# The last matrix product of a decoder layer: eight block products, or seven with sums of blocks

## The chip, the cores and the metric

One NeuronCore of a Trainium2 chip runs the whole program. TensorE (PE) does the matrix products and has a separate row of the profile for its weight loads (PEld); VectorE (DVE) and ScalarE (ACT) do the elementwise work; GpSimd (POOL) does little here, and SyncE (SP) issues most of the DMA transfers. The metric is the device time of one execution in microseconds (us): the median over the runs.

## The reference

One layer of a decoder with 512 positions and 1024 channels, in fp32. Four mixers give one 512-channel branch each. What follows them matters here:

```python
merged = jnp.sum(jax.nn.sigmoid(mg.reshape(B, S, N_BRANCHES, D)) * proj, axis=2)
return x + merged @ w_out
```

`mg` are gate columns of the input projection, `proj` the four branches after their own projection. `merged` is 512x1024, `w_out` 1024x1024. The products are to have nearly the accuracy of fp32.

## The kernel before

**Three matmuls for one.** Each operand of a matrix product is split into a rounded part `hi` (fp32r) and the rest `lo`; a product is hi\*hi + lo\*hi + hi\*lo, three matmuls. For a block of weights this costs a cast on ACT (`hi_cast`, L159) and a subtraction on DVE (L175, L1254 or L1396).

**The gates as seven products.** For the last three branches, `merge(n, ...)` computes the gate columns with the generator `seven()` (L1257). It cuts both operands into 2x2 blocks and replaces the eight block products by seven, of sums and differences of blocks. The sums of weight blocks are made by DVE in `add` (L1304, target `tsum` or a block that is no longer needed). Six PSUM banks hold what accumulates (`x`, `z`, `y`, two each): `seed` copies bank x to bank y on ACT, `less` (L1296) subtracts y from a kept copy `c` into z on DVE, `after_s3` does so again (L1299). A product is 24 matmuls. With `early` true (branch 2) the product of block 12 with block 21 of the weights comes second, so that it lies between the first product and the first one that needs a sum. Two more matmuls open bank y. Behind each gate comes `project()` (L1022): 2 x 96 matmuls into bank pairs `pj`, after which DVE multiplies by the gate (`th`, L1341) and adds to `acc` (L1342). The order of branches is 2, 1, 3.

**The output projection.** `acc` is turned by 32 transposes on PE (`turn`, L1383) through banks `tr`; ACT writes `mh` (L1386), DVE writes `ml` (L1387). Eight weight half-blocks of 1024 columns (`wo_split`) are split one by one, and `out_step` (L1405 to L1407) issues 192 matmuls of 128x512, first for the left half of the columns, then for the right. The rows of `x` come in eight DMAs of 256 KB on ACT's queue (`residual`, L1411). For every finished bank DVE adds them (L1415), and SP stores the result (L1416).

**What sets the order.** Generators hand out work in small steps (`yield`), `run` and `fill` take steps from them, and a scheduler orders the instructions of each engine. Each engine then works through its own list strictly in order. A raw block of weights has a limited number of slots (four under `raw`, five under `raw2`), so a load starts when an earlier block has been read.

Of the kernel before, what the change touches and what calls it, by code (L numbers as in the profile page):

```python
# [9 lines left out]
F32 = mybir.dt.float32  # L10
F32R = mybir.dt.float32r
# [50 lines left out]
def f32(ap):  # L62
    return ap.bitcast(F32)
# [3 lines left out]
def tile_hybrid_layer(ctx: ExitStack, tc: tile.TileContext, x, xT, units, small, bsp, out):  # L67
# [1067 lines left out]
    def sg_mix(dq):  # L1135
        wsh, wsl, bs, vnh, vnl = sg_setup(dq)
        for p_ in range(4):
            for b2 in range(2):
# [4 lines left out]
                for bb in range(2):  # L1143
# [5 lines left out]
                mx = accp.tile([P, S], F32, tag="tm", bufs=3, name=f"mx{p_}{b2}")[:, 0:256].rearrange("p (b t) -> p b t", b=2)  # L1149
# [9 lines left out]
    tmp_pool[:] = [accp, "tm"]  # L1159
    cnt["act"] = 0  # L1160
    later(*silu("gc", y["c"], (1, 3)), merge_plain(0, y["a"]))
    for i in range(4):
# [41 lines left out]
    def x_ops():  # L1204
# [11 lines left out]
        c = mp.tile([P, 1024], F32, name="xs").rearrange("p (k s) -> p k s", k=4)  # L1216
# [27 lines left out]

    def blocks(n):

        return {c: [half(*at, f"mg{n}{int(c[1]) - 1}.{int(c[0]) - 1}", h) for h in range(2)]
                for c, at in (("11", (wp, "raw", 4)), ("21", (wp, "raw", 4)), ("12", (mq, "raw2", 5)),
                              ("22", (mq, "raw2", 5)))}

    def weights(name, raw):
        w = wpair(name, 0)
# [4 lines left out]
    def seven(raws, ops, kt, emit, nm, early, beside):  # L1257

        nh = kt // 2
        b12, b11, b21, b22 = (raws[c] for c in ("12", "11", "21", "22"))  # L1260
        acc_ = {w: [zbank(f"{nm}{w}{p}") for p in range(2)] for w in "xzy"}
        cb = {}

        def product(w, op, src, first, then, made=None):
            hi_op, lo_op = ops[op]
            for h in range(nh):
                wt = made[h] if made else weights(f"{nm}{w}{op}", src[h])
# [17 lines left out]

        def seed(p, ps):
            if len(opened) < 2:
                opened.append(PE.matmul(acc_["y"][p], lhsT=xh[:, 0, 0:P], rhs=xh[:, 0, :], start=True, stop=True))
            ACT.copy(acc_["y"][p], ps)

        def keep(p, ps):
            cb[p] = accp.tile([P, S], F32, tag="th", bufs=4, name=f"{nm}c{p}")
            ACT.copy(cb[p], ps)

        def less(p, ps):
# [8 lines left out]
                DVE.tensor_tensor(dst[h], a[h], b[h], op=ALU.add)  # L1304

        def c11():
            return product("x", "12", b21, False, lambda p, ps: emit(p, 0, ps))
# [19 lines left out]
    def merge(n, yt, ths, first=False):  # L1327
# [16 lines left out]
        yield from seven(head if first else blocks(n), xo, 4, gate, f"mg{n}", first, y_split())  # L1344
        for c in range(2):
            yield from project(n, c, yh, yl, add)

# [10 lines left out]
    dqs.close()  # L1358
    mq = pool("mq")
    cnt["act"] = 1  # L1360
    head = blocks(2)
    head["w"] = [weights("mg2", raw) for raw in head["11"]]
    run(xg)
    drain()
# [1 line left out]
    psum_close("z")  # L1366
    psum_open("z")
    ps_["nz"] = 8
    ths = [tile8("th0"), ylp.tile([P, 4, S], F32, tag="vd", bufs=1, name="th1")]
# [7 lines left out]
    def turn(tp):  # L1377

        for kk in range(4):
            b = zbank(f"tr{tp}{kk}").rearrange("p (k t) -> p k t", k=2)  # L1380
            for k in range(2):
                for t in range(2):
                    PE.transpose(b[:, k, t * P:(t + 1) * P],  # L1383
                                 acc[:, 2 * tp + t, (2 * kk + k) * P:(2 * kk + k + 1) * P], identf)
            at = (slice(None), slice(2 * kk, 2 * kk + 2), slice(256 * tp, 256 * tp + 256))
            ACT.activation(mh[at], b, AF.Copy, scale=0.25)  # L1386
            DVE.scalar_tensor_tensor(ml[at], b, 0.25, f32(mh[at]), op0=ALU.mult, op1=ALU.subtract)  # L1387

    def wo_split(c, q):
        raw = half(*((wp, "raw", 4) if q % 2 else (mq, "raw2", 5)), f"wo{c}.{q // 2}", q % 2)  # L1390
        if c == 0 and q < 3:
            w = mp.tile([P, 2, 1024], F32R, tag=("s1", "s2", "s4")[q], bufs=1, name=f"wo{q}")
        else:
            w = wpair(f"wo{c}", q)
        hi_cast(w[:, 0, :], raw)
        DVE.tensor_tensor(w[:, 1, :], raw, f32(w[:, 0, :]), op=ALU.subtract)  # L1396
        return w[:, 0, :], w[:, 1, :]

    def out_step(pos, w, q, t):
        hi, lo = w  # L1400
        ts_ = slice(t * P, (t + 1) * P)
        for k2 in range(2):
            k = 2 * q + k2
            ws = slice(k2 * S, (k2 + 1) * S)
            PE.matmul(pos, lhsT=mh[:, k, ts_], rhs=hi[:, ws], start=k == 0, stop=False)  # L1405
            PE.matmul(pos, lhsT=ml[:, k, ts_], rhs=hi[:, ws], start=False, stop=False)  # L1406
            PE.matmul(pos, lhsT=mh[:, k, ts_], rhs=lo[:, ws], start=False, stop=k == KD - 1)  # L1407

    def residual(c, t):
        r = accp.tile([P, S], F32, tag="th", bufs=4, name=f"xr{c}{t}")  # L1410
        nc.scalar.dma_start(r, x[t * P:(t + 1) * P, c * S:(c + 1) * S])  # L1411
        return r

    def store(c, t, pos, r):
        DVE.tensor_tensor(r, pos, r, op=ALU.add)  # L1415
        DMA.dma_start(out[t * P:(t + 1) * P, c * S:(c + 1) * S], r)  # L1416

    turn(0)
    ws_ = {}
    for c in range(2):  # L1420
        pos = [zbank(f"out{c}{t}") for t in range(4)] if c else []
        xr_ = [residual(c, t) for t in range(4)]
        if c == 0:
            for tp in range(2):
                pos += [zbank(f"out0{2 * tp + t}") for t in range(2)]
                for q in range(4):
                    if tp == 0:
                        ws_[q] = wo_split(0, q)
                    for t in (2 * tp, 2 * tp + 1):
                        out_step(pos[t], ws_[q], q, t)  # L1430
                    if tp == 0 and q == 0:
                        turn(1)
                for t in (2 * tp, 2 * tp + 1):
                    store(0, t, pos[t], xr_[t])
        else:
            for q in range(4):
                w = wo_split(1, q)
                for t in range(4):
                    out_step(pos[t], w, q, t)
            for t in range(4):  # L1440
                store(1, t, pos[t], xr_[t])
    psum_close("z")


# [81 lines left out]
```

## Time and profile before

| | |
|---|---|
| time, median of 3 runs | 746.86 us (745.25 to 747.06) |
| the profiled execution | 745.62 us |
| its span, first to last instruction | 743.7 us |
| PE busy | 718.1 us, 97% of the span |
| DVE busy | 547.0 us, 74% |
| ACT busy | 356.6 us, 48% |
| last projection, 670.69 to 692.45 us | PE busy 21.76 of 21.76 us |
| output projection, 692.45 to 740.05 us | PE busy 47.60 of 47.60 us, DVE 15.27, ACT 7.18 |
| from there to the end | 3.65 us |

The profiled execution took 1.92 us beside its span and is 1.24 us under the median. Matmuls overlap: one of 128x512 is shown with about 0.39 us and starts about 0.23 us after the one before, so the distance of the starts tells what it costs.

### The profile page before, as it was taken

Reading aid. Unit: us, or ns where it says so; the run is one execution under the profiler, and the core shown is the slowest. Engines: PE = TensorE matmul, PEld = TensorE weight load, DVE = VectorE, ACT = ScalarE, POOL = GpSimd, SP = SyncE. Lnnn points to the kernel's source line nnn. Section 1 sums busy time; section 2 is a strip of 40 time slices with the busy share of each in tenths; the row PEclk is TensorE's granted clock in tenths of the full one; section 3 lists DMA queues with packets and bytes.
Section 4 is the critical chain, followed back from the end, with each engine's and each line's share of the span. In section 5 each row is a group of like instructions: output and inputs, shape, how many; then the busy total and the mean of one; then the engine's idle time right before and its main releaser. Section 6 shows DMA issues by size and latency. Waiting matters only on the chain.

```text
span 743.7 us, 9597 instructions
## 1 busy us (share of the span) xinstructions
PE 718.1 (97%) x3387; PEld 575.3 (77%) x3387; DVE 547.0 (74%) x1014; ACT 356.6 (48%) x731; POOL 185.5 (25%) x235
## 2 busy tenths in 40 slices
PE   8999999988999999999999999999999999999998
PEld 6878777766777787777777677788788888888886
DVE  5798757877568547978687999899768858965622
ACT  4422655655644136766576592433552551663210
POOL 5253644364444113233325333100000000000000
PEclk9999999999999999999999999999999999999999
DMA  8622311111113431100101133225432243143031
GB/s 312 216 69 101 115 56 58 57 57 58 63 51 105 151 113 57 58 30 29 57 30 32 55 113 100 85 85 198 134 122 85 83 140 111 65 141 112 0 114 56
DMA packets 20496, 68.35 MB, mean 92 GB/s; under 512 B 2400, under 2 KB 2528, under 8 KB 20448
## 3 DMA queue, kind: packets, MB, share of 16 engines
q1 hardware_dynamic: 19008, 65.28, 25.8%
q10 hardware_dynamic: 1440, 2.46, 1.0%
q8 instruction: 26, 0.43, 0.2%
q14 instruction: 22, 0.18, 0.1%
HBM read 65.64 MB, written 2.10 MB: 91 GB/s over the span
## 4 chain that ended last, share of the span: by engine, by line
PE 65%; DVE 17%; issue 7%; ACT 5%; POOL 5%; DMA 1%; SPq 0%; POOLq 0%; ACTq 0%; DVEq 0%
PE tb L573 3%; PE pj L1034 3%; PE pj L1035 3%; PE pj L1036 3%; PE out L1405 2%; PE out L1406 2%; PE out L1407 2%; PE o_s L586 1%; PE o_s L587 1%; PE z_va L212 1%; PE z_va L210 1%; DMA xr<-in_xT_dram 1%; PE z_va L211 1%; PE z_xb L189 1%; PE z_xb L190 1%
## 5 line engine op out<-in xcount | busy, mean ns | idle before, releaser
L1034 PE MATMUL pj<-w_wb,yh 128*128 128x512 f32 x128 | 49.9, 390 | 0.9 <-ACT tm L1006 0.9
L1035 PE MATMUL pj<-w_wb,yl 128*128 128x512 f32 x128 | 49.8, 389 | 0.0
L1036 PE MATMUL pj<-w_wb,yh 128*128 128x512 f32 x128 | 49.8, 389 | 0.0
L578 ACT CAST ph_a<-tb 128x256 fp32r<-128x256 f32 x40 | 14.8, 371 | 32.5 <-PE tb L573 30.1
L579 DVE TENSOR_TENSOR pl_a<-tb,ph_a 128x256 fp32r<-128x256 f32 x40 | 16.9, 421 | 17.1 <-ACT ph_a L578 16.9
L1034 PEld LDWEIGHTS pj<-w_wb,yh 128*128 128x128 f32 x128 | 24.0, 188 | 6.3 <-ACT tm L1006 1.3
L175 DVE TENSOR_TENSOR w_wb<-r_wb,w_wb 128x1024 fp32r<-128x1024 f32 x16 | 19.5, 1221 | 12.4 <-ACT w_wb L159 12.4
L1036 PEld LDWEIGHTS pj<-w_wb,yh 128*128 128x128 f32 x128 | 24.0, 188 | 5.1
L1035 PEld LDWEIGHTS pj<-w_wb,yl 128*128 128x128 f32 x128 | 24.0, 188 | 4.9
L562 POOL TENSOR_SCALAR p_w<-p_w,nm_w 128x128 f32<-128x128 f32 (+3 forms) x32 | 19.0, 612 | 31.8 <-DVE nm_w L559 18.1
L1415 DVE TENSOR_TENSOR xr<-out,xr 128x512 f32<-128x512 f32 x8 | 5.5, 692 | 27.1 <-PE out L1407 27.1
L562 POOL TENSOR_SCALAR p_s<-p_s,nm_s 128x128 f32<-128x128 f32 (+3 forms) x32 | 16.5, 533 | 35.6 <-DVE nm_s L559 21.7
L562 POOL TENSOR_SCALAR p_a<-p_a,nm_a 128x128 f32<-128x128 f32 (+3 forms) x32 | 20.2, 650 | 6.9 <-DVE nm_a L557 4.9
L579 DVE TENSOR_TENSOR pl_s<-tb,ph_s 128x256 fp32r<-128x256 f32 x40 | 16.3, 418 | 6.5 <-ACT ph_s L578 6.4
L578 ACT CAST ph_s<-tb 128x256 fp32r<-128x256 f32 x40 | 14.3, 371 | 13.5 <-PE tb L573 13.4
L554 ACT ACTIVATE p_w<-p_w,nm_w 128x512 f32<-128x512 f32 (+3 forms) x32 | 17.9, 561 | 5.9 <-DVE nm_w L552 5.8
L579 DVE TENSOR_TENSOR pl_w<-tb,ph_w 128x256 fp32r<-128x256 f32 x40 | 16.3, 421 | 5.9 <-ACT ph_w L578 5.5
L573 PE MATMUL tb<-identf,p_a 128*128 128x128 f32 x80 | 16.1, 281 | 3.7 <-DVE pl_a L579 1.6
L554 ACT ACTIVATE p_a<-p_a,nm_a 128x512 f32<-128x512 f32 (+3 forms) x32 | 17.8, 556 | 4.0 <-DVE nm_a L552 3.8
L578 ACT CAST ph_w<-tb 128x256 fp32r<-128x256 f32 x40 | 14.2, 371 | 10.9 <-PE tb L573 10.2
L159 ACT CAST w_wb<-r_wb 128x1024 fp32r<-128x1024 f32 x12 | 12.6, 1048 | 13.4 <-PE pj L1036 10.8
L554 ACT ACTIVATE p_s<-p_s,nm_s 128x512 f32<-128x512 f32 (+3 forms) x32 | 17.8, 559 | 2.1 <-DVE nm_s L552 2.1
(910 smaller groups left out, 2514.8 us busy)
## 6 DMA issues: line engine op xcount, KB each, us to landing
r_wb<-in_units_dram SPq DMA_DIRECT2D x16, 512.0 KB, 3.5
xt<-in_x_dram SPq DMA_DIRECT2D x4, 512.0 KB, 8.0
r_ga<-in_units_dram SPq DMA_DIRECT2D x4, 512.0 KB, 3.5
r_gd<-in_units_dram SPq DMA_DIRECT2D x4, 512.0 KB, 3.6
r_ud<-in_units_dram SPq DMA_DIRECT2D x4, 512.0 KB, 3.6
r_gc<-in_units_dram SPq DMA_DIRECT2D x4, 512.0 KB, 3.5
r_xb<-in_units_dram SPq DMA_DIRECT2D x4, 512.0 KB, 3.5
r_gb<-in_units_dram SPq DMA_DIRECT2D x4, 512.0 KB, 3.7
```

The lines of the kernel that those rows point to most:

```text
L175: DVE.tensor_tensor(w[:, 1, :], raw, f32(w[:, 0, :]), op=ALU.subtract)
L554: ACT.activation(pi, pi, AF.Exp, scale=-1.0, bias=nm[:, i:i + 1], accum_out=nm[:, 4 + i:5 + i])
L562: POOL.tensor_scalar(pi, pi, nm[:, 8 + i:9 + i], 0.0, op0=ALU.mult, op1=ALU.add)
L573: PE.transpose(t_[:, c * P:(c + 1) * P], u.p[:, OFF[i] + j * P:OFF[i] + (j + 1) * P], identf)
L578: ACT.copy(ph[:, c:c + 256], t_)
L579: DVE.tensor_tensor(pl_[:, c:c + 256], t_, f32(ph[:, c:c + 256]), op=ALU.subtract)
L1034: PE.matmul(banks[t], lhsT=yh[:, k, ts_], rhs=hi[:, cs], start=k == 0, stop=False)
L1035: PE.matmul(banks[t], lhsT=yl[:, k, ts_], rhs=hi[:, cs], start=False, stop=False)
L1036: PE.matmul(banks[t], lhsT=yh[:, k, ts_], rhs=lo[:, cs], start=False, stop=k == 3)
L1405: PE.matmul(pos, lhsT=mh[:, k, ts_], rhs=hi[:, ws], start=k == 0, stop=False)
L1406: PE.matmul(pos, lhsT=ml[:, k, ts_], rhs=hi[:, ws], start=False, stop=False)
L1407: PE.matmul(pos, lhsT=mh[:, k, ts_], rhs=lo[:, ws], start=False, stop=k == KD - 1)
```

## The change

The output projection goes through `seven()` with the four 512x512 blocks of `w_out` (`blocks("wo")`) and with the blocks of the merged result. For that:

- Per bank of the transposes the kernel keeps the merged values in fp32 as well (`mt`, `m21`), forms `s1`, `m3`, `s2` and `s4` as sums and differences of blocks, and splits each into an operand pair (`pair`: ACT copy, DVE subtraction).
- The sums of weight blocks are made as for the gates, four pairs of 1024-column additions.
- The blocks 11 and 21 of `w_out` are split during the last `project`; 21 goes to two slots of its own, and `run(last_merge, ...)` sets after which steps.
- The eight tiles of the output are emitted by the products in the order in which they are finished.
- The rows of `x` are fetched by eight DMAs on SP's queue into the slots of the last branch's operand (`res`).
- The pool of `th` and `tm` is closed before the gates, and one for the copies `c` opened in its place.

```diff
     thc.close()
+    keepp = pool("keepp", side="right")
...
-    for n, yt in ((2, y["c"]), (1, y["b"]), (3, ug)):
+    for n, yt in ((2, y["c"]), (1, y["b"])):
         run(merge(n, yt, ths, n == 2))
+    last_merge = merge(3, ug, ths)
+    run(last_merge, 56 + 16 + 9)
+    wraw = blocks("wo")
+    wraw["w"] = [weights("wo11", raw) for raw in wraw["11"]]
+    run(last_merge, 2)
+    wraw["w21"] = [weights("wo21", wraw["21"][0], ylp.tile([P, 2, 1024], F32R, tag="z8", bufs=1, name="w_wo21"))]
+    run(last_merge, 2)
+    wraw["w21"].append(weights("wo21", wraw["21"][1], keepp.tile([P, 2, 1024], F32R, name="w_wo21h1")))
+    run(last_merge)
...
+    for c, t0 in ((0, 0), (1, 2), (1, 0), (0, 2)):
+        for t in (t0, t0 + 1):
+            DMA.dma_start(res[c][:, t, :], x[t * P:(t + 1) * P, c * S:(c + 1) * S])
...
+    def pair(nm, src, w):
+        hi, lo = (w[:, j, :].rearrange("p (k s) -> p k s", k=4) for j in range(2))
+        ACT.copy(hi, src)
+        DVE.tensor_tensor(lo, src, f32(hi), op=ALU.subtract)
+        mo[nm] = (hi, lo)
...
+    lowb = [turn(0, kk, bank) for kk, bank in enumerate(tb + ob["z"])]
+    highb = [turn(1, kk, bank) for kk, bank in enumerate(ob["y"])]
+    for kk in range(4):
+        turn_split(0, kk, lowb[kk])
+    for kk in range(2):
+        ACT.activation(mt[:, at2[kk], :], lowb[kk], AF.Copy, scale=0.25)
+    for kk in range(2):
+        ACT.activation(m21[:, at2[kk], :], highb[kk], AF.Copy, scale=0.25)
+
+    def store(t, c, src):
+        r = res[c][:, t, :]
+        DVE.tensor_tensor(r, src, r, op=ALU.add)
         DMA.dma_start(out[t * P:(t + 1) * P, c * S:(c + 1) * S], r)
...
+    go = seven(wraw, mo, 4, store, "wo", True, iter(()), ob)
+    run(go, 1)
+    highb = [turn(1, 2 + kk, bank) for kk, bank in enumerate(tb)]
+    for kk in range(2):
+        DVE.scalar_tensor_tensor(s1[:, at2[kk], :], highb[kk], -0.25, m21[:, at2[kk], :], op0=ALU.mult, op1=ALU.add)
+    pair("s1", s1, operand("s1"))
+    for kk in range(2):
+        ACT.activation(mt[:, at2[2 + kk], :], lowb[2 + kk], AF.Copy, scale=0.25)
+        turn_split(1, 2 + kk, highb[kk])
+    run(go, 9)
+    DVE.tensor_tensor(m3, m11, m21, op=ALU.subtract)
+    DVE.tensor_tensor(m11, s1, m11, op=ALU.subtract)
+    pair("s2", m11, operand("s2"))
+    run(go, 12)
+    pair("s3", m3, mid("ms3"))
+    run(go, 8)
+    DVE.tensor_tensor(m12, m12, m11, op=ALU.add)
+    pair("s4", m12, operand("s4"))
+    run(go)
```

The functions `wo_split`, `out_step` and `residual`, and the loop that calls them, go. In `seven()` the subtraction `less` is L1299 after the change (L1296 before), the sums are L1307, the splits L1256.

Three places in the order of the instructions. The first is DVE's list during the last `project`, before the change (`w_wb` are the weights that this projection still needs, `wo` those of the output):

```order
L175 TENSOR_TENSOR w_wb_5990<-r_wb_5988,w_wb_5990 128x1024 [waits DMAHW7_49,PE_49,Activation_49]
L1396 TENSOR_TENSOR wo_6141<-r_wo0.01_6139,wo_6141 128x1024 [waits DMAHW6_49,Activation_49]
L175 TENSOR_TENSOR w_wb_6019<-r_wb_6017,w_wb_6019 128x1024 [waits DMAHW0_49,Activation_49]
L1341 SCALAR_TENSOR_TENSOR th_4848<-th_4848,pj_5914 128x512 [waits PE_49]
L1341 SCALAR_TENSOR_TENSOR th_4848<-th_4848,pj_5915 128x512 [waits PE_49]
```

and after it:

```order
L1307 TENSOR_TENSOR tsum<-r_wo0.00_6032,r_wo1.00_6040 128x1024 [waits DMAHW6_49,DMAHW2_49]
L175 TENSOR_TENSOR w_wb_5997<-r_wb_5995,w_wb_5997 128x1024 [waits DMAHW5_49,PE_49,Activation_49]
L1307 TENSOR_TENSOR tsum<-r_wo0.01_6034,r_wo1.01_6042 128x1024 [waits DMAHW7_49,DMAHW3_49]
L1307 TENSOR_TENSOR r_wo1.00_6040<-r_wo1.00_6040,r_wo1.10_6044 128x1024 [waits DMAHW0_49,DVE_49]
L1307 TENSOR_TENSOR r_wo1.01_6042<-r_wo1.01_6042,r_wo1.11_6046 128x1024 [waits DMAHW1_49,DVE_49]
L175 TENSOR_TENSOR w_wb_6026<-r_wb_6024,w_wb_6026 128x1024 [waits DMAHW6_49,Activation_49]
L1344 SCALAR_TENSOR_TENSOR th_4855<-th_4855,pj_5921 128x512 [waits PE_49]
```

Four additions that wait for loads of `w_out` (DMAHW) now stand ahead of the last split that the projection needs and ahead of the first gate multiplication.

The second place is PE's list at the start of the output projection, before:

```order
L1383 MATMUL tr_6077<-identf,acc 128x128 x4
L1405 MATMUL out_6092<-wo_6096,mh 128x512 [waits Activation_49]
L1405 MATMUL out_6093<-wo_6096,mh 128x512
L1383 MATMUL tr_6111<-identf,acc 128x128 [waits DVE_49]
L1383 MATMUL tr_6111<-identf,acc 128x128 x2
L1406 MATMUL out_6092<-wo_6096,ml 128x512 [waits DVE_49]
```

and after (the banks `outz` and `outy` serve as transpose banks first):

```order
L1405 MATMUL outy_6101<-identf,acc 128x128 x4
L1279 MATMUL outx_6096<-w_wo_6048,mh 128x512 [waits DVE_49,Activation_49]
L1281 MATMUL outx_6096<-w_wo_6048,ml 128x512 [waits DVE_49]
L1283 MATMUL outx_6096<-w_wo_6048,mh 128x512
L1279 MATMUL outx_6096<-w_wo_6048,mh 128x512
L1405 MATMUL tr_6094<-identf,acc 128x128 [waits Activation_49]
```

24 instead of 16 transposes stand ahead of the first matmul of the product, and the last eight, which write the first two banks a second time, wait for ACT.

The third place is DVE's list in the output projection, after the change, up to the subtraction `less` (`ms` are the operand pairs, `w_woys` the split sums of weight blocks, `woc` the kept copy):

```order
L1417 TENSOR_TENSOR ms_6256<-m_6093,ms_6256 128x1024
L1438 TENSOR_TENSOR resh<-outx_6097,resh 128x512 [waits DMAHW0_49,PE_49]
L1307 TENSOR_TENSOR tsum<-tsum,r_wo1.10_6044 128x1024 [waits DVE_49]
L1307 TENSOR_TENSOR tsum<-tsum,r_wo1.11_6046 128x1024 [waits DVE_49]
L1458 TENSOR_TENSOR mt<-mt 128x1024
L1256 TENSOR_TENSOR w_woys_6269<-tsum,w_woys_6269 128x1024 [waits Activation_49]
L1256 TENSOR_TENSOR w_woys_6284<-tsum,w_woys_6284 128x1024 [waits Activation_49]
L1417 TENSOR_TENSOR ms_6295<-mt,ms_6295 128x1024 [waits Activation_49]
L1307 TENSOR_TENSOR tsum<-tsum,r_wo0.10_6036 128x1024 [waits DVE_49]
L1307 TENSOR_TENSOR tsum<-tsum,r_wo0.11_6038 128x1024 [waits DVE_49]
L1299 TENSOR_TENSOR outz_6098<-woc_6254,outy_6100 128x512 [waits PE_49]
L1299 TENSOR_TENSOR outz_6099<-woc_6265,outy_6101 128x512 [waits PE_49,Activation_49]
```

Before the change this stretch of DVE's list held eight `ml`, three splits and the additions of the residual rows; now 25 operations stand between the last `acc` addition and `less`, 10 of 512 elements (six `ml`, two into `mu`, two residual additions) and 15 of 1024. SP's list has the eight loads of `x` behind all loads of `w_out` and ahead of the stores.

## Rows read from the trace of the kernel before

**Rows 1.** The page's part 1: busy time, share of span, instructions.

```profile
PE 718.1 (97%) x3387; PEld 575.3 (77%) x3387; DVE 547.0 (74%) x1014; ACT 356.6 (48%) x731; POOL 185.5 (25%) x235
```

**Rows 2.** Busy time by stretch: branch 2's gates, last projection, output projection; columns ahead.

```profile
core 0: us, PE busy (x) PEld busy (x) DVE busy (x) ACT busy (x) POOL busy (x), PEclk, DMA share, GB/s
511.68:550.99 39.31, 38.93 (x171) 31.76 (x170) 29.83 (x30) 21.17 (x26) 0.00 (x0) 1.00 0.35 118
670.69:692.45 21.76, 21.76 (x97) 17.97 (x96) 13.77 (x18) 5.65 (x6) 0.00 (x0) 1.00 0.23 80
692.45:740.05 47.60, 47.60 (x225) 39.31 (x223) 15.27 (x22) 7.18 (x11) 0.00 (x0) 1.00 0.16 55
```

**Rows 3.** Timeline of PE, output stage's start: start, duration, instruction, count.

```profile
692.22 0.39 PE L1036 MATMUL pj<-w_wb,yh 128*128 128x512 f32 x1
692.45 1.91 PE L1383 MATMUL tr<-identf,acc 128*128 128x128 f32 x16
694.25 0.73 PE L1405 MATMUL out<-wo,mh 128*128 128x512 f32 x2
```

**Rows 4.** Timeline of PE and DVE at the end; in brackets, idle time and releaser.

```profile
739.43 0.39 PE L1406 MATMUL out<-w_wo,ml 128*128 128x512 f32 x1
...
739.66 0.39 PE L1407 MATMUL out<-w_wo,mh 128*128 128x512 f32 x1
740.09 0.69 DVE L1415 TENSOR_TENSOR xr<-out,xr 128x512 f32<-128x512 f32 x1 [0.67 <-PE out L1407]
```

**Rows 5.** Timeline of PE: branch 2's gates begin, their projection begins.

```profile
511.68 0.39 PE L1277 MATMUL mg2x<-w_mg,xh 128*128 128x512 f32 x1
...
551.01 0.39 PE L1034 MATMUL pj<-w_wb,yh 128*128 128x512 f32 x1
```

**Rows 6.** Timeline around branch 2's subtraction `less`.

```profile
533.76 1.29 DVE L1296 TENSOR_TENSOR mg2z<-mg2c,mg2y 128x512 f32<-128x512 f32 x2
...
534.57 0.19 PEld L1277 LDWEIGHTS mg2y<-w_mg2ys,xs 128*128 128x128 f32 x1 [0.78 <-issue]
534.60 0.47 PE L1277 MATMUL mg2y<-w_mg2ys,xs 128*128 128x512 f32 x1 [0.38 <-DVE mg2z L1296]
```

**Rows 7.** Timeline of ACT and DVE as the output projection begins.

```profile
693.26 1.29 DVE L1342 TENSOR_TENSOR acc<-acc,th 128x512 f32<-128x512 f32 x2
...
693.61 2.04 ACT L1386 ACTIVATE mh<-tr 128x512 fp32r<-128x512 f32 x4
...
694.46 2.48 DVE L1387 SCALAR_TENSOR_TENSOR ml<-tr,mh 128x512 fp32r<-128x512 f32 x4
```

**Rows 8.** Timeline of DVE in branch 2's gates.

```profile
519.09 0.69 DVE L1333 TENSOR_TENSOR yl<-y_c,yh 128x512 fp32r<-128x512 f32 x1
519.69 1.22 DVE L1254 TENSOR_TENSOR w_mg2zs<-tsum,w_mg2zs 128x1024 fp32r<-128x1024 f32 x1
520.94 1.22 DVE L1304 TENSOR_TENSOR tsum<-tsum,r_mg21.10_4781 128x1024 f32<-128x1024 f32 x1
```

**Rows 9.** Timeline of DVE in branch 1's projection, which began at 610.85.

```profile
612.02 1.22 DVE L1304 TENSOR_TENSOR tsum<-r_mg30.00_5648,r_mg31.00_5656 128x1024 f32<-128x1024 f32 x1 [1.39 <-DMA r_mg30.00_5648<-in_units_dram]
...
614.96 1.23 DVE L1304 TENSOR_TENSOR tsum<-r_mg30.01_5650,r_mg31.01_5658 128x1024 f32<-128x1024 f32 x1 [0.57 <-DMA r_mg30.01_5650<-in_units_dram]
616.10 1.22 DVE L1304 TENSOR_TENSOR r_mg31.00_5656<-r_mg31.00_5656,r_mg31.10_5660 128x1024 f32<-128x1024 f32 x1
617.24 1.22 DVE L1304 TENSOR_TENSOR r_mg31.01_5658<-r_mg31.01_5658,r_mg31.11_5662 128x1024 f32<-128x1024 f32 x1
...
619.51 1.28 DVE L1341 SCALAR_TENSOR_TENSOR th<-th,pj 128x512 f32<-128x512 f32 x2
```

**Rows 10.** Timeline of DVE in the last projection, which began at 670.69.

```profile
678.56 1.28 DVE L1341 SCALAR_TENSOR_TENSOR th<-th,pj 128x512 f32<-128x512 f32 x2
```

**Rows 11.** DMA issues from 560 us on: KB each, median us to landing.

```profile
r_mg30.00_5648<-in_units_dram SPq DMA_DIRECT2D x1, 512.0 KB, 3.5
...
r_wo1.00_6260<-in_units_dram SPq DMA_DIRECT2D x1, 512.0 KB, 6.1
```

More of the change, by code (lines that the diff above doesn't have):

```diff
@@ L996, in tile_hybrid_layer @@
     acc = accp.tile([P, 4, D], F32, name="acc")
+    thc = ExitStack()
+    thp = pool("thp", thc, side="right")
     def merge_plain(n, yt):
@@ L1157, in sg_mix @@
                 yield 0.8
-    tmp_pool[:] = [accp, "tm"]
+    tmp_pool[:] = [thp, "tm"]
     cnt["act"] = 0
@@ L1245, in blocks, with weights @@
     def blocks(n):
-        return {c: [half(*at, f"mg{n}{int(c[1]) - 1}.{int(c[0]) - 1}", h) for h in range(2)]
+        return {c: [half(*at, f"{n}{int(c[1]) - 1}.{int(c[0]) - 1}", h) for h in range(2)]
                 for c, at in (("11", (wp, "raw", 4)), ("21", (wp, "raw", 4)), ("12", (mq, "raw2", 5)),
                               ("22", (mq, "raw2", 5)))}
-    def weights(name, raw):
-        w = wpair(name, 0)
+    def weights(name, raw, w=None):
+        w = wpair(name, 0) if w is None else w
         hi_cast(w[:, 0, :], raw)
@@ L1255, in weights, with seven @@
         return w
-    def seven(raws, ops, kt, emit, nm, early, beside):
+    def seven(raws, ops, kt, emit, nm, early, beside, banks=None):
         nh = kt // 2
         b12, b11, b21, b22 = (raws[c] for c in ("12", "11", "21", "22"))
-        acc_ = {w: [zbank(f"{nm}{w}{p}") for p in range(2)] for w in "xzy"}
+        acc_ = banks or {w: [zbank(f"{nm}{w}{p}") for p in range(2)] for w in "xzy"}
         cb = {}
@@ L1266, in product @@
             for h in range(nh):
-                wt = made[h] if made else weights(f"{nm}{w}{op}", src[h])
+                wt = made[h] if made and h < len(made) else weights(f"{nm}{w}{op}", src[h])
                 hi, lo = wt[:, 0, :], wt[:, 1, :]
@@ L1287, in seed @@
             if len(opened) < 2:
-                opened.append(PE.matmul(acc_["y"][p], lhsT=xh[:, 0, 0:P], rhs=xh[:, 0, :], start=True, stop=True))
+                opened.append(PE.matmul(acc_["y"][p], lhsT=ops["11"][0][:, 0, 0:P], rhs=raws["w"][0][:, 0, 0:S], start=True,
+                                        stop=True))
             ACT.copy(acc_["y"][p], ps)
         def keep(p, ps):
-            cb[p] = accp.tile([P, S], F32, tag="th", bufs=4, name=f"{nm}c{p}")
+            cb[p] = keepp.tile([P, S], F32, tag="kept", bufs=3, name=f"{nm}c{p}")
             ACT.copy(cb[p], ps)
@@ L1306, in c11 @@
         def c11():
-            return product("x", "12", b21, False, lambda p, ps: emit(p, 0, ps))
+            return product("x", "12", b21, False, lambda p, ps: emit(p, 0, ps), raws.get("w21"))
         t_ = [tsum[:, h, :] for h in range(nh)]
@@ L1342, in add @@
             DVE.tensor_tensor(a, a, th, op=ALU.add)
-        yield from seven(head if first else blocks(n), xo, 4, gate, f"mg{n}", first, y_split())
+        yield from seven(head if first else blocks(f"mg{n}"), xo, 4, gate, f"mg{n}", first, y_split())
         for c in range(2):
@@ L1360, in tile_hybrid_layer @@
     cnt["act"] = 1
-    head = blocks(2)
+    head = blocks("mg2")
     head["w"] = [weights("mg2", raw) for raw in head["11"]]
@@ L1374, in tile_hybrid_layer @@
+    run(last_merge, 2)
+    wraw["w21"].append(weights("wo21", wraw["21"][1], keepp.tile([P, 2, 1024], F32R, name="w_wo21h1")))
+    run(last_merge)
     mh = xp.tile([P, KD, S], F32R, tag="xh", bufs=1, name="mh")
     ml = xp.tile([P, KD, S], F32R, tag="xl", bufs=1, name="ml")
[L1377 to L1415, printed above, removed]
-        DMA.dma_start(out[t * P:(t + 1) * P, c * S:(c + 1) * S], r)
[L1418 to L1441, printed above, removed]
@@ new lines, in tile_hybrid_layer @@
+    mt, mu = (tile8(nm)[:].rearrange("p a (b s) -> p (a b) s", b=2) for nm in ("mt", "mu"))
+    m3 = mp.tile([P, 1024], F32, tag="xs", bufs=1, name="m3").rearrange("p (k s) -> p k s", k=4)
+    m11, m12, m21, s1 = mt[:, 0:4, :], mt[:, 4:8, :], mu[:, 0:4, :], mu[:, 4:8, :]
+    tb = [zbank(f"tr{j}") for j in range(2)]
+    ob = {w: [zbank(f"out{w}{p}") for p in range(2)] for w in "xzy"}
+    res = [accp.tile([P, 4, S], F32, tag="y" + w, bufs=1, name=f"res{w}") for w in "hl"]
+    for c, t0 in ((0, 0), (1, 2), (1, 0), (0, 2)):
+        for t in (t0, t0 + 1):
+            DMA.dma_start(res[c][:, t, :], x[t * P:(t + 1) * P, c * S:(c + 1) * S])
@@ new lines, in turn, with turn_split @@
+    def turn(tp, kk, bank):
+        b = bank.rearrange("p (k t) -> p k t", k=2)
+        for k in range(2):
+            for t in range(2):
+                PE.transpose(b[:, k, t * P:(t + 1) * P],
+                             acc[:, 2 * tp + t, (2 * kk + k) * P:(2 * kk + k + 1) * P], identf)
+        return b
+    def turn_split(tp, kk, b):
+        at = (slice(None), slice(2 * kk, 2 * kk + 2), slice(256 * tp, 256 * tp + 256))
+        ACT.activation(mh[at], b, AF.Copy, scale=0.25)
+        DVE.scalar_tensor_tensor(ml[at], b, 0.25, f32(mh[at]), op0=ALU.mult, op1=ALU.subtract)
@@ new lines, in pair, with operand @@
+    def pair(nm, src, w):
[3 more added lines that the diff above has]
+        mo[nm] = (hi, lo)
+    def operand(nm):
+        return mp.tile([P, 2, 1024], F32R, tag=nm, bufs=1, name="m" + nm)
+    k1, k2 = slice(0, 4), slice(4, 8)
+    mo = {"11": (mh[:, k1, LOW], ml[:, k1, LOW]), "12": (mh[:, k2, LOW], ml[:, k2, LOW]),
+          "22": (mh[:, k2, HIGH], ml[:, k2, HIGH])}
@@ new lines, in tile_hybrid_layer @@
+    at2 = [slice(2 * kk, 2 * kk + 2) for kk in range(4)]
+    lowb = [turn(0, kk, bank) for kk, bank in enumerate(tb + ob["z"])]
[9 more added lines that the diff above has]
+        DVE.tensor_tensor(r, src, r, op=ALU.add)
+        DMA.dma_start(out[t * P:(t + 1) * P, c * S:(c + 1) * S], r)
```

10 lines of the change are left out of this document (6 added, 4 removed).

## The prediction

> **What bounds the kernel now.** I read the page's busy shares first. PE is busy for 97% of the span, DVE for 74% [rows 1]; whatever the change does, it must show in PE's list. The shares are an average, so the second view is the busy time by stretch [rows 2]: in the output projection PE works 47.60 of 47.60 us, with DVE at 15.27 and ACT at 7.18; in the projection ahead of it 21.76 of 21.76, with DVE at 13.77. The granted clock is 1.00 in all of them, so a matmul has one price. That price comes from the stretch of the last projection: 96 matmuls of 128x512 from 670.69 to 692.45, 21.76 / 96 = 0.2267 us from start to start (the 0.39 in a row is latency, since starts lie 0.23 apart [rows 4]). The third view is the timeline at both ends of the stage. The transposes begin right behind the last matmul of the projection, 16 take 694.25 - 692.45 = 1.80, so 0.1125 each [rows 3]. The last matmul starts at 739.66; the final addition and its store follow [rows 4].
>
> So the stage before is a sum: 739.66 + 0.23 - 692.45 = 47.44 us. Of these 192 x 0.2267 = 43.53 are products, 32 x 0.1125 = 3.60 transposes, and 0.31 are left for waits. PE's number of instructions times its pitch is the whole stage; no other engine ends it.
>
> **What the change removes and adds on PE.** Seven products of 24 matmuls and two that open bank y: 170 instead of 192. The transposes remain 32. 22 x 0.2267 = 4.99 us go. Other stages of PE's list stay as they are; one cast in branch 2's gates moves behind a copy, with 24 matmuls of another product as cover, and I set it at nothing.
>
> **What it adds in waits.** The trace has the very same generator in the same early order, branch 2's gates. Its 170 matmuls run from 511.68 to 551.01 [rows 5], 39.33 us where 170 x 0.2267 = 38.54 would do, so 0.79 of waits. The largest is at `less`: PE needs z free of its subtraction, and the row of the weight load shows 0.78 idle, that of the matmul 0.38 [rows 6]. I take 0.5 for it, and 0.1 for the copy of x to y.
>
> A wait of another kind is at the start. The last eight transposes write banks that ACT must have read into `mh` and `mt`. ACT's four `mh` start at 693.61 and take 0.51 each [rows 7]; the first `mt` then ends near 693.61 + 5 x 0.51 = 696.2. PE comes there at 692.45 + 24 x 0.1125 + 4 x 0.2267 = 696.06. I take 0.25; ends: 0 when ACT begins earlier, since the first transposes it reads are over soon after 693, and 0.75 when one more ACT operation slips in. `ml`, which the second matmul of the product needs, is close to a wait and I count none for it: DVE starts it at 694.46 [rows 7], 0.7 later it is done, at 695.15, and PE wants it at 695.38.
>
> Sum: 170 x 0.2267 + 3.60 + 0.25 + 0.1 + 0.5 = 42.99, against 47.44: -4.45. With branch 2's own measured length it is 39.33 + 3.60 + 0.25 = 43.18: -4.26. I take -4.4.
>
> **What hides the rest.** DVE has 25 operations between the last `acc` addition and `less`. Start to start, one of 512 elements costs 0.60 (519.09 to 519.69 [rows 8]), one of 1024 costs 1.14 (616.10 to 617.24 [rows 9]). 10 x 0.60 + 15 x 1.14 = 23.1 us from 694.46: DVE is ready for `less` at 717.6. PE has the first bank of that product finished six matmuls before its end: 692.45 + 3.60 + 98 x 0.2267 + 0.35 = 718.6, less 1.36, plus the latency of 0.39 less 0.23, 717.4. So DVE works without a pause for 23 us and arrives within 0.2 of PE. This is the point on which the forecast rests; each further 1 us on DVE costs PE about 1 us, once. Behind `less` DVE has some 12.8 us of work (10 of 512, 6 of 1024) for 16.3 us of three products on PE, and catches up.
>
> In the last projection DVE gets five operations more (four sums, one more split): 5 x 1.14 = 5.7 us. Idle there are 21.76 - 13.77 = 8.0 [rows 2]; 2.3 remain. The same sums stand in branch 1's projection, for branch 3's gates: there DVE waits 1.39 and 0.57 for loads [rows 9], and its first gate multiplication comes 619.51 - 610.85 = 8.66 after the projection's start, against 678.56 - 670.69 = 7.87 without sums [rows 10]. That lateness of 0.8 fits into 2.3, so I set it at nothing; uncovered it is 0.8. The splits of blocks that PE needs are ahead of their matmuls by a whole product.
>
> ACT has 7.18 us in the stage [rows 2] and gets 11 operations of 1024 elements (casts and operand copies) and 10 of 512 (copies of banks). Even at DVE's pitches [rows 8, 9] that is 11 x 1.14 + 10 x 0.60 = 18.5 us more in 43: not a bound. The eight loads of `x` leave ACT's queue and stand on SP's behind the weights, ahead of the stores. They start at the end of the projection, the first is needed some 13 us later; even the slowest landing here, 6.1 us [rows 11], leaves time. The stores wait on DVE as before. The end has the same form, one addition of 0.69 and one store behind the last matmul [rows 4]: no change.
>
> Profiled execution: 745.62 - 4.4 = 741.2. It lies 1.24 under the median of 746.86, so for the median 746.86 - 4.4 = 742.5.
>
> **Where a rule of the skill speaks against it.** The rows show DVE starting an operation 0.08 before the end shown for the one ahead: 1.14 start to start at 1.22 duration [rows 9]. Only an operation that reads what the one ahead wrote starts later, 1.25 (519.69 to 520.94 [rows 8]). The Trainium skill, "VectorE: DVE Perf Modes", section "The DRAIN you can't avoid", says that the next operation does not start until the pipe is empty, though it also says that one that isn't held starts earlier. By that sentence DVE's chain would take the full duration at every step, the second rival below; the trace agrees for operations that depend on the one ahead, and not for the others.
>
> **Rivals.**
>
> *The sums of DVE at the price of dependent operations.* Most of the 25 read what DVE or ACT has just written. At full price, 10 x 0.69 + 15 x 1.25 = 25.65 instead of 23.1: `less` is 2.5 later, of which 0.2 are slack. Saving 4.4 - 2.3 = 2.1: 744.8. For it: the 1.25 of [rows 8]. Against it: the scheduler puts independent operations between the dependent ones, and the four sums of [rows 9] run at 1.14 though each waits on something.
>
> *Late weights.* The first sum waits for loads of `w_out` at the head of DVE's list. In branch 1's projection such loads took 3.5 us and DVE waited 1.39 + 0.57 for them; loads of `w_out` took up to 6.1 [rows 9, 11]. With 2.6 us more, the first wait becomes 4.0 and swallows the second: 2.0 more of waiting, where 2.3 - 1.96 = 0.3 was free. DVE's chain starts 1.7 late, and `less` with it. Saving 2.7: 744.2. For it: the slow row belongs to just these blocks. Against it: those were loaded at other moments, in another order.
>
> *Slower.* The same head of DVE's list, with a price beyond the gain. Behind the sums stands the split of `w_wb` that PE needs for the second half of the projection, halfway at 681.6 (670.69 + 48 x 0.2267). If the loads of `w_out` come one behind the other, so that the last of the blocks needed lands 7 us later than in branch 1's projection, PE stands at the projection already and again at the output: 4.4 gained, 7 lost, 749.5. It decides from a delay of 4.4 + 2.2 = 6.6 on. For it: SP's list has seven blocks of `w_out` in a row, each behind a slot that DVE must free. Against it: the queue carries the same row of blocks for branch 3, and the wait there is 1.39.
>
> *No gain.* The end is set by something else than PE's number of matmuls. Nothing in [rows 2] speaks for it.
>
> **How the numbers follow.** A measurement of this kernel can tell 0.3%, 2.2 us: faster is under 744.6, slower over 749.1. The forecast has 0.67, with a range of its own from 741.5 (no waits at all, -5.3) to 744 (waits of 2.4); all of it is faster. The dependent price has 0.13, at the bound: 0.05 faster, 0.08 same. Late weights have 0.12: 0.08 faster, 0.04 same. Slower has 0.06. No gain has 0.02, half same, half slower. Together 0.80, 0.13, 0.07. The range goes from 740.9 (no waits, 741.5, and 0.6 for the spread of the runs) to 745.8, which takes in both middle rivals with 1 us more.
>
> **What would show it.** In the profile after: the stage from the first transpose to the last matmul 43.0 us instead of 47.4, at an unchanged pitch of 0.2267; a wait at `less` under 1 us; DVE without idle time from 694 to 717; the end as it was. A wait at `less` of 2 us or more with DVE busy all the way speaks for the dependent price; DVE idle on a `r_wo` load before the projection's gate multiplication, for late weights; PE idle within the last projection, for the slower case. Wrong altogether would be a stage longer than 45 us, or a pitch other than 0.2267.

## The result, and the profile after

The changed kernel takes 740.79 us (median of 6 runs, 740.59 to 741.43) against 746.41 (6 runs, 745.25 to 747.06): ratio 0.9927, 95% interval [0.9915, 0.9940]. The forecast was a time of 742.5, 4.4 us under the 746.86 of three runs; with three more runs the median of the kernel before is 746.41, and the saving is 5.6 us. The time lies 0.1 us under the lower end of the stated range, 740.9; as a share of the kernel before (740.9 / 746.86 = 0.9920, measured 0.9927) it lies inside. Taken again with five further runs the ratio was 0.9952 [0.9940, 0.9964], 3.6 us; the forecast lies between the two, and the sections below say what the difference is.

The page's busy shares, to set beside [rows 1]:

```profile
PE 713.5 (97%) x3365; PEld 570.6 (77%) x3365; DVE 571.9 (77%) x1039; ACT 370.3 (50%) x749; POOL 185.4 (25%) x235
```

PE has 22 instructions fewer and is 4.6 us less busy; DVE has 25 more and 24.9 us more work, ACT 18 more and 13.7. The span is 739.0 us, and the profiled execution took 740.70.

The windows of the profile after, as in [rows 2]: branch 2's gates, the last projection, the output projection to just behind its last matmul, and the rest (columns as there).

```profile
511.12:550.47 39.35, 38.97 (x172) 31.75 (x170) 29.82 (x29) 21.08 (x26) 0.00 (x0) 1.00 0.37 117
670.15:691.91 21.76, 21.76 (x97) 17.97 (x96) 19.36 (x23) 6.80 (x7) 0.00 (x0) 1.00 0.26 82
691.91:735.26 43.35, 43.17 (x203) 34.84 (x201) 37.64 (x44) 22.04 (x30) 0.00 (x0) 1.00 0.23 85
735.26:739.00 3.74, 0.00 (x1) 0.00 (x0) 0.69 (x1) 0.00 (x0) 0.00 (x0) 1.00 0.36 140
```

The first two stretches have the length they had. DVE's work in the last projection is 19.36 instead of 13.77, 5.6 more, and PE doesn't wait for it. The output projection is shorter, with DVE at 37.64 instead of 15.27.

The timeline of PE at its start and end (answers to [rows 3, 4]):

```profile
691.68 0.39 PE L1038 MATMUL pj<-w_wb,yh 128*128 128x512 f32 x1
691.91 1.03 PE L1405 MATMUL tr<-identf,acc 128*128 128x128 f32 x8
...
695.23 0.40 PE L1279 MATMUL outx<-w_wo,mh 128*128 128x512 f32 x1
695.66 1.15 PE L1405 MATMUL tr<-identf,acc 128*128 128x128 f32 x8
...
734.87 0.39 PE L1283 MATMUL outy<-w_woy,mh 128*128 128x512 f32 x1
```

By the same measure as in the forecast the stage is 734.87 + 0.23 - 691.91 = 43.19 us, 4.25 shorter than 47.44. The pitch is unchanged: 170 x 0.2267 + 3.60 = 42.13, and 1.06 are waits. The wait for the transpose banks is 695.66 - 695.23 - 0.23 = 0.20. Most of the others stand at `less`. The timeline of DVE's list from its start, and of PE and DVE at `less`:

```profile
693.92 1.28 DVE L1412 SCALAR_TENSOR_TENSOR ml<-tr,mh 128x512 fp32r<-128x512 f32 x2
...
696.61 1.29 DVE L1446 SCALAR_TENSOR_TENSOR mu<-tr,mu 128x512 f32<-128x512 f32 x2 [0.21 <-ACT mu L1434]
...
716.33 1.22 DVE L1307 TENSOR_TENSOR tsum<-tsum,r_wo0.11_6038 128x1024 f32<-128x1024 f32 x1
...
717.46 0.69 DVE L1299 TENSOR_TENSOR outz<-woc,outy 128x512 f32<-128x512 f32 x1
...
717.85 0.39 PE L1283 MATMUL outy<-w_woys,ms 128*128 128x512 f32 x1
...
718.30 0.47 PE L1279 MATMUL outy<-w_woys,ms 128*128 128x512 f32 x1
718.35 0.70 DVE L1299 TENSOR_TENSOR outz<-woc,outy 128x512 f32<-128x512 f32 x1 [0.20 <-PE outy L1283]
718.60 0.40 PE L1281 MATMUL outy<-w_woys,ms 128*128 128x512 f32 x1
718.95 1.22 DVE L1256 TENSOR_TENSOR w_woys<-r_wo1.00_6040,w_woys 128x1024 fp32r<-128x1024 f32 x1
719.10 0.50 PE L1279 MATMUL outy<-w_woys,ms 128*128 128x512 f32 x1
719.44 0.39 PE L1281 MATMUL outy<-w_woys,ms 128*128 128x512 f32 x1
```

Every distance of two matmul starts above 0.227 in these rows is a wait: 0.22 between 717.85 and 718.30, then 0.07, 0.27 and 0.11, together 0.67. The first `less` has no idle time ahead: DVE came to it straight from a sum of weights. The second bank y had to be free before the third matmul of the next product, and only two matmuls stood in between, since the third one of each group of three (L1283) wants the split that DVE makes at 718.95.

In the last projection DVE's waits for loads are nearly what they were in branch 1's [rows 9]:

```profile
671.42 1.23 DVE L1307 TENSOR_TENSOR tsum<-r_wo0.00_6032,r_wo1.00_6040 128x1024 f32<-128x1024 f32 x1 [1.49 <-DMA r_wo0.00_6032<-in_units_dram]
...
674.45 1.23 DVE L1307 TENSOR_TENSOR tsum<-r_wo0.01_6034,r_wo1.01_6042 128x1024 f32<-128x1024 f32 x1 [0.67 <-DMA r_wo0.01_6034<-in_units_dram]
...
679.00 1.28 DVE L1344 SCALAR_TENSOR_TENSOR th<-th,pj 128x512 f32<-128x512 f32 x2
```

1.49 and 0.67 where branch 1 had 1.39 and 0.57, and the first gate multiplication comes 8.85 after the projection's start instead of 7.87 [rows 10]. The rows of `x` landed in 5.8 and 5.9 us (median) instead of 2.8 on ACT's queue; no residual addition waited for one.

### The profile page after: what moved, and what is told of

The parts are those of the page before. It is cut to its first block, busy times and chain, and to the rows that moved or that the text cites. A ratio compares the mean times of both kernels' runs of the same rounds, so it can differ in the third digit from the quotient of the medians.

```text
span 739.0 us, 9603 instructions
## 1 busy us (share of the span) xinstructions
PE 713.5 (97%) x3365; PEld 570.6 (77%) x3365; DVE 571.9 (77%) x1039; ACT 370.3 (50%) x749; POOL 185.4 (25%) x235
## 4 chain that ended last, share of the span: by engine, by line
PE 65%; DVE 16%; issue 7%; ACT 6%; POOL 4%; DMA 1%; SPq 0%; POOLq 0%; DVEq 0%; ACTq 0%
PE tb L573 3%; PE pj L1038 3%; PE pj L1037 3%; PE pj L1036 3%; PE z_va L210 1%; PE z_va L212 1%; PE o_s L587 1%; DMA xr<-in_xT_dram 1%; PE z_va L211 1%; PE z_qa L211 1%; PE o_s L586 1%; PE z_qa L212 1%; PE z_qa L210 1%; PE z_xb L189 1%; PE z_xb L190 1%
## 5 line engine op out<-in xcount | busy, mean ns | idle before, releaser
L573 PEld LDWEIGHTS tb<-identf,p_a 128*128 128x128 f32 x80 | 9.1, 140 | 11.8 <-DVE pl_a L579 6.2
```

Source lines behind the costliest of these rows:

```text
L573: PE.transpose(t_[:, c * P:(c + 1) * P], u.p[:, OFF[i] + j * P:OFF[i] + (j + 1) * P], identf)
```

## The experiments

**The changed kernel again, beside its parts.** No edit.

> The changed kernel once more, beside the three below. My account (the stage is PE's matmuls times 0.2267 plus 1.05 of waits, 4.25 us shorter than before) expects 4.0 to 4.6 us under the kernel before, so that the rest of the first difference of 5.6 (746.41 to 740.79) was scatter between executions. The rival, that something ahead of the output projection became faster too (the profile of after is 0.56 us earlier when branch 2's gates begin), expects 5 to 6 us again.

Measured: 741.94 against 745.22, ratio 0.9952 [0.9940, 0.9964]. Its stage runs from 693.66 to 736.62, that is 43.19 us again, with the same 1.06 of waits, though it begins 1.75 later than in the first profile. In the stage my account holds. In time it came out a little low: 3.3 us by the two medians and 3.6 by the ratio, where I had expected 4.0 to 4.6; the interval, 2.7 to 4.5 us, takes in most of that and leaves out the rival's 5 to 6.

**The pools alone.** In the kernel before:

```diff
-                th = accp.tile([P, S], F32, tag="th", bufs=4, name=f"tm{n}{c}{t}")
+                th = thp.tile([P, S], F32, tag="th", bufs=4, name=f"tm{n}{c}{t}")
...
+    thc.close()
+    keepp = pool("keepp", side="right")
...
-        r = accp.tile([P, S], F32, tag="th", bufs=4, name=f"xr{c}{t}")
+        r = keepp.tile([P, S], F32, tag="xr", bufs=4, name=f"xr{c}{t}")
```

> The kernel before with the change of pools alone: th and tm in a pool of their own that is closed before the gates, the copies c and the residual rows in the pool opened in its place; output projection as before. My account: no difference (within 0.5 us of before), since no instruction is added or removed. The rival (the other places in memory speed up what comes ahead of the output projection): 0.5 to 1.2 us faster, with branch 2's gates starting 0.5 us earlier than 511.68 in the profile.

Measured: 744.96 against 745.22, ratio 0.9998 [0.9990, 1.0007]. Branch 2's gates start at 512.45, later than the 511.68 of [rows 5], not earlier. The start of that stage lies between 510.50 and 512.90 in the ten profiles of the two kernels and these variants, in no relation to what was changed: that is the scatter of what comes before, and the first comparison had it in its favour.

**The rows of `x` alone.** In the kernel before:

```diff
-    def residual(c, t):
-        r = accp.tile([P, S], F32, tag="th", bufs=4, name=f"xr{c}{t}")
-        nc.scalar.dma_start(r, x[t * P:(t + 1) * P, c * S:(c + 1) * S])
-        return r
+    res = [accp.tile([P, 4, S], F32, tag="y" + w, bufs=1, name=f"res{w}") for w in "hl"]
+    for c_ in range(2):
+        for t_ in range(4):
+            DMA.dma_start(res[c_][:, t_, :], x[t_ * P:(t_ + 1) * P, c_ * S:(c_ + 1) * S])
+
+    def residual(c, t):
+        return res[c][:, t, :]
```

> The kernel before with the rows of x alone changed: eight loads on SP's queue behind the last loads of w_out, into the slots of the last branch's operand; 192 matmuls as before. My account: no difference (within 0.5 us), since DVE waits for PE at every residual addition and never for a row of x. The rival (part of the gain is ACT's queue freed of eight DMA issues, or SP's queue made longer costs something at the stores): 0.5 to 1.5 us either way.

Measured: 745.68 against 745.22, ratio 1.0007 [0.9998, 1.0015]; the stage is 692.67 to 739.90 + 0.23, 47.46 us. Neither part has a share in the gain that these runs can show (the intervals reach to 0.75 us of gain for the pools and 0.15 for the rows); what remains is the seven products.

**One product less.**

```diff
-        yield from product("y", "22", t_, False, lambda p, ps: emit(2 + p, 0, ps))
+        if banks:
+            for p in range(2):
+                emit(2 + p, 0, acc_["y"][p])
+        else:
+            yield from product("y", "22", t_, False, lambda p, ps: emit(2 + p, 0, ps))
```

> The changed kernel without the last of the seven products (24 matmuls and the split of its weights); four of the eight tiles of the output lack its part. My account (the stage is matmuls times pitch): 24 x 0.2267 = 5.44 us shorter, stage 37.75 instead of 43.2, the end behind the last matmul as before, so 5.2 to 5.7 below the changed kernel's time. The rival (the end is set by the rows of x, the stores or DVE's list, and the seventh product lies beside them): 2 us or less.

Measured: 735.81 against 745.90, ratio 0.9870 [0.9854, 0.9886], 10.1 below the kernel before. The timeline of PE, first transposes and last matmul:

```profile
692.45 1.04 PE L1409 MATMUL tr<-identf,acc 128*128 128x128 f32 x8
...
729.98 0.39 PE L1283 MATMUL outz<-w_wozs,ms 128*128 128x512 f32 x1
```

729.98 + 0.23 - 692.45 = 37.76 us, 5.43 under 43.19 (expected 5.44). From the last matmul's start to the end of the span it is 4.12 (4.13 with all seven). Matmuls times pitch is the stage. (The changed kernel was not run beside this run, nor beside any of those below but the one with less work ahead of `less`; their times stand against the kernel before, and the comparison with the changed kernel is that of the stages.)

**More work on DVE, first try.** Four operations more, tied to `less`:

```diff
+        if nm in ("s2", "s3"):
+            for _ in range(2):
+                last["more"] = DVE.tensor_tensor(lo, src, f32(hi), op=ALU.subtract)
...
         def less(p, ps):
-            DVE.tensor_tensor(acc_["z"][p], cb[p], ps, op=ALU.subtract)
+            with tc.issue_after(last["more"].ins if banks else last["rest"].ins):
+                DVE.tensor_tensor(acc_["z"][p], cb[p], ps, op=ALU.subtract)
```

> The changed kernel with four more DVE operations of 1024 elements (subtractions of the operand pairs s2 and s3 done three times), which the subtraction less has to await; in DVE's list 27 instead of 25 operations then stand ahead of less, another one between its two halves and one more behind, ahead of the split that the product s3 needs. My account (DVE's list has no pause from the transposes to less and arrives there together with PE, so every further operation ahead of it is paid by PE): less begins 2 x 1.14 = 2.3 us later, the split for s3 4 x 1.14 = 4.6 later, of which some matmuls that don't need it cover a part; the stage is 3 to 4.2 us longer than 43.2, the time 3 to 4.2 above the changed kernel's, nearly that of the kernel before. The rival (PE's count of matmuls alone sets the stage, DVE has room to spare): 43.2 us and no difference.

Measured: 747.35 against 745.90, ratio 1.0020 [1.0010, 1.0031]. The stage is 49.13 us, 5.9 longer where I had expected 3 to 4.2. I had overlooked two things. The further operations came ahead of the split of the weights for s2 as well, and PE waited there first:

```profile
714.99 0.40 PE L1281 MATMUL outy<-w_woys,ms 128*128 128x512 f32 x1
717.59 0.80 PE L1283 MATMUL outy<-w_woys,ms 128*128 128x512 f32 x1 [2.20 <-DVE w_woys L1256]
718.18 0.63 PE L1279 MATMUL outy<-w_woys,ms 128*128 128x512 f32 x1
```

and behind that wait the matmuls came every 0.43 us for a while, at a granted clock of 0.53 (the column ahead of the last two):

```profile
717.50:721.10 3.60, 3.51 (x8) 2.80 (x9) 3.44 (x4) 0.00 (x0) 0.00 (x0) 0.53 0.00 0
```

So the experiment mixes three costs: the late split, the clock, and the later waits at `less`. I made a cleaner one.

**More work on DVE, at `less` alone.** Two operations more, and nothing else moved in DVE's list:

```diff
+        if nm == "s4":
+            for _ in range(2):
+                last["more"] = DVE.tensor_tensor(lo, src, f32(hi), op=ALU.subtract)
...
-    run(go, 8)
+    run(go, 5)
```

with `less` tied to them as above.

> The changed kernel with two more DVE operations of 1024 elements just ahead of the subtraction less (the subtraction of the operand pair s4 done three times), all else of DVE's list in its order, and behind everything that the product s2 needs. My account (DVE's list has no pause up to less): less begins 2 x 1.14 = 2.3 us later and PE waits there 2.3 us more, stage 45.5 instead of 43.2. If a wait of that length brings the granted clock to its lower level, as the profile of the kernel with four more showed behind a wait of 2.4 us (0.53 in a stretch of 3.6 us), another 1.5 to 2 come on top: 47 to 47.5, and a stretch at about 0.5 behind the wait. The rival (DVE has room to spare): 43.2, no difference.

Measured: 743.61 against 745.29, ratio 0.9978 [0.9966, 0.9990]: half of the gain or more is gone. PE at `less`:

```profile
717.26 0.39 PE L1283 MATMUL outy<-w_woys,ms 128*128 128x512 f32 x1
719.97 0.47 PE L1279 MATMUL outy<-w_woys,ms 128*128 128x512 f32 x1 [2.32 <-DVE outz L1300]
```

The wait is 719.97 - 717.26 - 0.23 = 2.48, 2.26 more than 0.22, as two steps of 1.14 make it. DVE's list has no room ahead of `less`. The windows ahead of the wait, in it, behind it, and then to the end (columns as in [rows 2]):

```profile
714.00:717.60 3.60, 3.60 (x17) 2.68 (x15) 3.60 (x4) 1.20 (x2) 0.00 (x0) 1.00 0.00 0
717.60:720.20 2.60, 0.28 (x2) 0.26 (x2) 2.60 (x4) 1.04 (x1) 0.00 (x0) 1.00 0.00 0
720.50:723.90 3.40, 3.40 (x9) 2.63 (x8) 3.32 (x3) 0.00 (x0) 0.00 (x0) 0.50 0.00 0
724.00:738.00 14.00, 14.00 (x63) 11.38 (x61) 7.79 (x10) 3.16 (x3) 0.00 (x0) 1.00 0.19 75
```

The granted clock, in the column ahead of the last two, is 0.50 behind the wait, the lower of the two levels, and 1.00 again 3.4 us later. Eight matmuls in that stretch start about 0.2 us late each, 1.6 in all. The stage has 4.60 of waits in all (46.7 us, a little under the 47 to 47.5 expected), 3.5 more than 1.06: 2.3 for DVE's two operations and 1.6 for the clock, less some 0.4 of the waits between the two halves of `less`. That is the profiled execution, at 743.61. Its fall of the clock did not come in each: a stretch of 3.4 us at 0.50 takes 0.0023 off an execution's mean granted clock, and three of the seven have a mean of 0.999 or 1.000, too high for it. These three are the fastest, 742.85 to 743.38 us; the other four took 743.61 to 745.22.

**Less work ahead of `less`.** The sums for the last product go behind it, the first split for s3 ahead of it:

```diff
-        add(t_, t_, b21)
+        if not banks:
+            add(t_, t_, b21)
...
         yield from product("y", "s3", b12, False, after_s3)
+        if banks:
+            with tc.issue_after(last["less"].ins):
+                add(t_, t_, b21)
```

and in `weights` the second split for s3 is put behind `less` in the same way.

> The changed kernel with DVE's list changed around the subtraction less: the two additions of block 21 to tsum come after it, the split of the first half of the weights for the product s3 before it, the second half's behind it, so that 24 instead of 25 operations are ahead. My account: DVE arrived 0.3 us after PE there (its list had no pause) and the split stood behind the subtraction, so PE lost 0.22 + 0.07 + 0.27 + 0.11 = 0.67 us at this place; of that 0.4 to 0.65 go, the stage is 42.6 us instead of 43.2, and the time is 0.4 to 0.7 below the changed kernel's. The rival (the wait at less is the latency from one engine to the other, whatever DVE does): the 0.67 stay, no difference; a second rival, that the operations moved behind it make PE wait later: the stage gets longer by up to 1 us.

Measured: 740.62 against 745.22, ratio 0.9939 [0.9927, 0.9952], beside 0.9952 for the changed kernel on the same chip. In times the intervals overlap; in the profile the place is clean. DVE and PE there:

```profile
714.81 1.22 DVE L1257 TENSOR_TENSOR w_woys<-r_wo1.00_6040,w_woys 128x1024 fp32r<-128x1024 f32 x1
...
716.53 0.70 DVE L1301 TENSOR_TENSOR outz<-woc,outy 128x512 f32<-128x512 f32 x1 [0.51 <-PE outy L1285]
...
717.24 0.39 PE L1283 MATMUL outy<-w_woys,ms 128*128 128x512 f32 x1
717.47 0.39 PE L1285 MATMUL outy<-w_woys,ms 128*128 128x512 f32 x1
717.69 0.39 PE L1281 MATMUL outy<-w_woys,ms 128*128 128x512 f32 x1
717.89 0.70 DVE L1301 TENSOR_TENSOR outz<-woc,outy 128x512 f32<-128x512 f32 x1 [0.66 <-PE outy L1285]
```

DVE now waits 0.51 for PE, no matmul there starts more than 0.23 behind the one before, and the stage is 42.59 us. The 0.67 was DVE's lateness and the order of its list, not a price of the subtraction. The stage of this version is the shortest of the kernels with seven products; in time only its median is under the changed kernel's (740.62 against 741.94).

**The other order of products.**

```diff
-    go = seven(wraw, mo, 4, store, "wo", True, iter(()), ob)
+    go = seven(wraw, mo, 4, store, "wo", False, iter(()), ob)
```

> The changed kernel with the generator's other order: the product of block 12 of the merged result with block 21 of the weights comes after s2 instead of second (the scheduler spreads a few of its matmuls ahead of that). My account by the lists: s2 is reached 5.4 us earlier, when DVE has done 16 operations from the transposes on, 8 x 0.60 + 8 x 1.14 = 13.9 us, while PE has done 32 transposes and some 54 matmuls, 15.9 us less the 2.0 that DVE starts later, so they meet within 0.3; at less the moved product covers the wait of 0.67. The stage is 42.5 to 43.3, the time from 0.7 below to 0.1 above the changed kernel's. The rival (the early place is what gives DVE the time for its sums): PE waits 1 to 2.5 us at s2, and the stage is 44 to 45.5.

Measured: 741.25 against 745.90, ratio 0.9936 [0.9923, 0.9948]; stage 693.38 to 735.81 + 0.23, 42.66 us, waits 0.53. `less` begins at 715.55, PE goes on with the moved product until 719.72, and s2 begins at 709.12 with 0.10 and 0.11 us of waits. The place of that product early in the list isn't what lets DVE keep up; put later, it covers `less`. More than the place changed, though: the scheduler put seven matmuls of the moved product just ahead of and among the first of s2, and DVE has 21 operations ahead of `less` instead of 25. So this shows that the other order works as well, not which of the three does it.

## Why the prediction was right, and where it was off

*PE's count times its pitch.* Right: 22 matmuls fewer, 4.99 us. One product more out took 5.43 of the 5.44 it should.

*The sum of the stage.* 42.99 forecast, 43.19 measured; the waits were 1.06 instead of 0.85. The bank wait at the start was 0.20 (0.25 forecast), `less` and the two halves behind it 0.67 (0.5), the copy of x to y none (0.1), and 0.2 lie in small steps of under 0.1 in the first product. That the sum agrees to 0.2 is in part luck: the terms were off by 0.05 to 0.2 each, and not all to the same side.

*The step from the stage to the time.* This was the part that was off in the first comparison: 5.6 instead of 4.4. The stage gave 4.25 of it in both profiles of the changed kernel. The first pair of profiled executions, 745.62 and 740.70, is 4.92 apart: 0.54 more lie ahead of the stage (691.91 instead of 692.45), and the rest outside the span. The other 0.7 is where those two executions stand among their own: 0.79 under the median of six before, 0.09 under it after. The 0.54 doesn't come from the change as far as the runs tell: the pools alone and the rows alone make no difference, and in the second profile of the changed kernel the stage begins 1.2 later than before the change. So it was luck of the first comparison. Outside the span the change may have a share that the forecast didn't have: an execution took 1.67 to 1.79 us beside its span in all 41 listed runs with the output from products of sums, and up to 2.90 with the old one (over 1.79 in 23 of 70), 0.2 us on the mean. What makes it so was not looked into. A median of 3 to 6 runs of this kernel moves by about a microsecond.

*DVE without pause from the transposes to `less`.* Right but for two short stops: first `ml` 693.92, `less` 717.46, 23.5 us for 23.1. The 0.4 more are 0.3 ahead of `mu`, which waited for ACT (0.21 of it shown as idle), and 0.2 ahead of the first addition of residual rows. The rows of [rows 7] had `ml` at 694.46 with the stage beginning 0.54 later, so the chain began where it was said to. DVE came to `less` 0.5 us after PE had the bank ready instead of the 0.2 that was counted: in the version with less work ahead of `less`, where DVE waits for PE, it begins 25.01 us after the first transpose (716.53 - 691.52), here 25.55. Of that lateness 0.22 came through as PE's first wait.

*"Each further 1 us on DVE costs PE about 1 us, once."* Right for PE's wait itself, 2.26 us for 2.28, but in the profile not for what it costs: the stage became 3.5 longer, as the clock fell behind the wait. The forecast's rival of dependent operations, 2.5 us on DVE, was priced at 2.3; an estimate from this profile is up to 3.5, 746 instead of 744.8, little gain. It didn't come about: the sums and splits went at 1.14 where the operation ahead was another (716.33 to 717.46), as in [rows 9], and none of the 25 stands right behind one whose result it reads or whose source it overwrites. The 1.25 of [rows 8] was also read wrongly: that sum doesn't read what the split ahead of it wrote (`w_mg2zs`), it writes into the sums that the split reads (`tsum`). The sentence of the Trainium skill that was weighed there, "VectorE: DVE Perf Modes", section "The DRAIN you can't avoid", that an operation waits for the pipe of the one ahead to empty, is not what this list shows: `less` starts 0.09 us before the end shown for the sum ahead of it (716.33 + 1.22 against 717.46).

*Late weights.* Waits of 1.49 and 0.67, 0.1 more each than for the blocks of branch 3. The lateness of the first gate multiplication was 1.0 instead of 0.8, and it was hidden, but with little left: of 8.0 us of idle time in the projection 2.4 remain, some 2 of them in these two waits. The slower rival, a delay of 6.6, didn't come near. That a late landing alone would do what was forecast for it wasn't tried.

*The residual rows and the end.* As forecast, nothing within the span. The loads became slower and were still early.

## What to carry to other kernels

Where PE is busy to the last tenth of a microsecond, count its instructions and multiply by the pitch; a product saved is worth its matmuls if the engine that makes the sums arrives in time. Count that engine's list up to the first place where PE needs something back from it, not its share of the stage: here it was 87% busy in the stage and yet nearly all of its room was behind that place. Operations that nobody needs yet should stand behind such a place in the list.

## What the runs showed of the hardware

A wait of TensorE of about 2.4 us was followed by a stretch at half the granted clock in both profiles that had one: 0.53 over 3.6 us behind 2.37 us (four more operations), 0.50 over 3.4 us behind 2.48 us (two more). The 128x512 matmuls started every 0.43 us in it instead of every 0.227. Waits up to 0.89 in the output projection of the same runs left the clock at 1.00. So a wait can cost 1.6 us more than its length. It need not: three of seven executions with two more operations, and one of nine with four more (745.73 us, the fastest, mean clock 1.000), have a mean clock too high for such a stretch. And the length of the wait alone doesn't decide. At about 154 us, far ahead of the stages looked at here, TensorE stands idle for 1.1 us in all ten profiles; in three of them (the rows of `x` alone, four more operations, the other order) a stretch of 3.4 us at 0.50 lies there, in the other seven the clock stays at 1.00.
